# A two-layer encoder on one core: the second layer's plain x scaled at the layer's head, the decays loaded first, and the token sublayers in another order

## The chip, the cores and the metric

The kernel runs on one NeuronCore of a Trainium2 chip. The number of interest is the device time in microseconds (us) of one execution. The core has five engines that run side by side, each with its own instruction stream: TensorE (PE; its weight loads are listed as PEld), VectorE (DVE), ScalarE (ACT), GpSimd (POOL) and SyncE (SP). Data moves between the chip's memory (HBM) and the on-chip memory by DMA, issued here from the queues of SP and POOL. Matmul results land in eight PSUM banks.

## The reference

The trunk has two layers, on 512 tokens of width 1024. Each layer has a token sublayer and a channel sublayer, each followed by a residual addition with a factor alpha and a layer norm:

```python
for i in range(DEPTH):
    proj = x @ w_in[i]
    q_na, k_na, v_na, q_r, k_r, v_r, g_r, gate_a, gate_b = jnp.split(proj, IN_SPLITS, axis=-1)
    ya = neighbourhood_attention(...)          # 8 heads of 64, windows of 8 x 16
    yb = bidirectional_retention(...)          # 4 heads, group norm, times silu(g)
    merged = sigmoid(gate_a) * (ya @ w_branch_a[i]) + sigmoid(gate_b) * (yb @ w_branch_b[i])
    y = merged @ w_out[i]
    x = layer_norm(DEEPNORM_ALPHA * x + y, ln1_g[i], ln1_b[i])
    ffn = conv_glu_ffn(x, w_up[i], conv_w[i], conv_b[i], w_down[i])
    ple = jax.nn.sigmoid(x @ w_ple_gate[i]) * (p[i] @ w_ple_proj[i])
    x = layer_norm(DEEPNORM_ALPHA * x + ffn + ple, ln2_g[i], ln2_b[i])
```

The retention decays come from the inputs by a logarithm of a sigmoid, computed on the chip.

## The kernel before

**Arithmetic.** All operands are float32. Each is split into a high part `hi` (a cast, on ScalarE) and the rest `lo` (a subtraction, on VectorE), and each product is made of three matmuls: hi by hi, hi by lo, lo by hi (`mm3`, L434 to L436). A weight tile of 128 x 1024 is loaded from `wpack` into `raw`, split by `split` (L178, L179) and used by 12 or 24 matmuls. An item marked `sent` is split in another way (L392 to L394): ScalarE writes hi and minus hi, and a DMA issued by POOL adds the weight onto the latter, so VectorE does nothing for it.

**Blocks with sums.** Large products are done as blocks with seven products instead of eight, from sums of quarters of the operands (kinds a, c, t1, t2, d, t3, t4). For the weights, quarters are added by DMAs that accumulate in the tile (`rawa`, POOL's queue, L342). For the activations, `quad_sums` forms sums and splits them on VectorE and ScalarE.

**The stream of weights.** `Stream` lists all weight tiles in the order of use; `get` prepares a few tiles ahead of the one in use, and loads further ahead. A tile goes into a small pool of three, or, where a tuple such as `VG_HELD` or `BB_HELD` names it, into the unit pool (30 units of 128 x 1024), which lets it be prepared earlier.

**A token sublayer.** The head (`vg`) runs the keys of `VG[l]`: blocks 0 to 3 (values and gates, keys such as 3a, 2c) and plain products (nq, nk: queries and keys of the attention; q, k: of the retention, with rotary). Generators hang on the keys by `at_key`, and each call of one is a step: sums of x, the split of the second half of x, the decays, the tables of constants. In the head the engines run in the order in which the program is written (`_Ordered`, whose calls appear as L109). After it come the fillers in the order of `FILL[l]`, between which the steps of the attention heads (`NA_AT`) and of the retention heads (`RET_AT`) are placed by slot; here a scheduler orders each engine's instructions. The filler `ba` is the attention's branch product; after the fillers, `bb` is the retention's branch product in a block of seven, merged with the gates M (L1178, L1179), and turned by transpositions (`turn`, L1134). Then `proj_ln` makes the output projection with eight weight tiles, adds the residual `xn` and does LN1 (L506, L509).

**Plain x.** The residual needs x by rows. In layer 0 it is an input. In layer 1 it is LN2's output: at the end of layer 0, `norm` normalises R, four tiles of 128 x 1024, and each is stored without scale and shift into `x_scr`. In layer 1, in the middle of `bb` (step `XN_AT`), `plain_x` loads the constants and the four tiles and multiplies and adds on VectorE:

```python
                    nc.sync.dma_start(z, (scr if l else x_nat)[t * P:(t + 1) * P, :])
                    ...
                        nc.vector.tensor_mul(z, z, g)
                        nc.vector.tensor_add(z, z, b)
```

The transposed x of layer 1 is made from R apart from this (`out_pair`, with scale and shift on ScalarE), the first half at the end of layer 0, the second by `pending` at the head of layer 1.

**The start.** The first loads, in SP's queue, are p and its weights, x and the weights of block 3; the decays `dl` and `zd` are loaded by a step of `second_half`, and a later step computes their logarithms on VectorE with small instructions (`decay_logs`).

**The channel sublayer** (`pg`, up and down projections) is not touched.

Of the kernel before, what the change touches and what calls it, by code (L numbers as in the profile page):

```python
# [37 lines left out]
FILL = (('2c', '3t2', '3d', 'nk1', 'vn', '3t3', '3t4', '2t1', 'nk2', '2t2', '2d', '2t3', '0a', 'nq2', 'k2', '0t1', '2t4', '0t2', '0d', '0t3', '1a', 'q0',  # L38
# [9 lines left out]
OUT_PREP = ((0, 1, 1, 1), (0, 1, 1, 1))  # L48
# [32 lines left out]
VG_EARLY = 'd'  # L81
VG_HELD = (('0c', '0t2', '1a', '1c', '1t2', '1t4', '2a', '2t4', '3t1', '3t2'),
 ('0a', '0c', '0d', '0t3', '1c', '1t4', '2a', '2c', '2t1', '2t3', '3a', '3c', '3d', '3t1', '3t2', '3t3'))
# [42 lines left out]
def trunk(tc, wpack, x_nat, x_tr, head, p_tr, rpb, decay, ln_par, ln_col, conv, cos_t, sin_t, dist, xi_d, zd, ident_d, out):  # L126
# [4 lines left out]
    with ExitStack() as es:  # L131
# [103 lines left out]
        def vg_items(l):  # L235

            by = {}
            for b, c0 in enumerate((0, 12, 52, 36)):
                pos = {(q, j): (l, c0 + 2 * i + j, 0, 1024) for i, q in enumerate("acbd") for j in range(2)}
                for it in block_items(pos, {k[1:]: up for k in VG_HELD[l] if k[0] == str(b)}, VG_EARLY, ON_CHIP[l][b]):  # L240
                    it.block = b
                    by.setdefault(f"{b}{it.kind}", []).append(it)
            return [it for k in (*VG[l], *FILL[l]) for it in (by[k] if k in by else plain_items(l, k))]
# [19 lines left out]
        def bb_items(l):  # L263

            pos = {(q, j): (l, 44 + 2 * i + j, 0, 1024) for i, q in enumerate("acbd") for j in range(2)}
            by = {}
            for it in block_items(pos, {k: up for k in BB_HELD[l]}, BB_EARLY[l]):
                by.setdefault(it.kind, []).append(it)
            return [it for k in BB for it in by[k]]
# [34 lines left out]
        class Stream:  # L304


            def __init__(self):
                self.seq = []
                for l in range(DEPTH):
# [4 lines left out]
                    for c in range(64, 72):  # L314
                        plain(c)
                    self.seq += pg_items(l)
                    for s, n in enumerate(SEGS):
# [245 lines left out]
        for kp in range(2):  # L563
            x_load(0, kp)
            ws.load(3 + kp)
        ws.load(5)
        for kp in range(2):
            x_load(1, kp)
# [42 lines left out]

        NDL = DEPTH * 8
        lgs = cp.tile([P, NDL], F32, name="lgs")
        dl = cp.tile([P, NDL], F32, name="dl_0")
        nlg = cp.tile([P, NDL], F32, name="nlg")
# [69 lines left out]
        gscr = dp.tile([2, T, D], F32, name="g_scr")  # L685
        pending = None

        for l in range(DEPTH):
# [6 lines left out]
            def block(lh, emit):  # L695
# [61 lines left out]
                return step  # L757

            stores = []

# [160 lines left out]
            def ret_head(h):  # L921
# [39 lines left out]
                for tq in range(2):  # L961
# [17 lines left out]
                    for i in range(2):  # L979
                        y = yb[:, 2 * tq + i, :]  # L980
                        nc.vector.scalar_tensor_tensor(y, ps[:, i * 256:(i + 1) * 256], mv[:, i, 0:1], gg(2 * tq + i),
                                                       op0=ALU.subtract, op1=ALU.mult)
                        nc.vector.tensor_scalar_mul(y, y, r[:, i:i + 1])
                yield
# [132 lines left out]
            def plain_x():  # L1117

                if l:
                    g, b = ln_consts(l - 1, 1)  # L1120
                for t in range(4):
                    z = unit_f("xn")
                    nc.sync.dma_start(z, (scr if l else x_nat)[t * P:(t + 1) * P, :])
                    xn.append(z)
                    if l:
                        nc.vector.tensor_mul(z, z, g)
                        nc.vector.tensor_add(z, z, b)

# [87 lines left out]
            for i in range(n1 - 1, n1 + 3):  # L1216
                at_key(i, sums)
            if l == 0:
                rest, first = second_half(), first_half()
                at_key("p1", first)  # L1220
                at_key(0, first)
                at_key(2, ple_keep(l))
                tab = tables()
                for i in REST_AT:
                    at_key(i, rest)
                for i in TABLES_AT:
                    at_key(i, tab)
            else:
                rest = pending(2, xt, xf)
                at_key(1, ple_keep(l))  # L1230
                for i in PEND_AT:
# [19 lines left out]
            def fillers():  # L1251
                F = FILL[l]
                for i, f in enumerate(F):
                    if f == "vn":
                        yield from na_v()
                        continue
# [363 lines left out]
            for s, n in enumerate(SEGS):  # L1620
# [178 lines left out]
                for k in BOUND if not last else ("t4a", "t4b"):  # L1799
# [7 lines left out]
                    else:  # L1807
# [5 lines left out]
                        if not last:  # L1813
                            norm(i)
                            nc.sync.dma_start(scr[i * P:(i + 1) * P, :], R[i])
# [133 lines left out]
```

## Time and profile before

| | |
|---|---|
| time, median of 3 runs | 1685.13 us (1683.48 to 1687.44) |
| the profiled execution | 1689.1 us, with a span of 1687.3 us from the first to the last instruction |
| mean granted TensorE clock | 0.997 |
| busy: PE, DVE, ACT, POOL | 1656.4, 1314.1, 996.3, 232.2 us |
| moved by DMA | 324.13 MB, 192 GB/s |

The page gives the busy time of each engine and its costliest groups of instructions. A query by stretches gives the busy time in each, so that a full engine in one stage is seen where the average hides it. The list of waits says which engine waited for which, and the instructions in order of time show in brackets how long an engine had been idle and what ended that. A matmul's row lasts longer than the distance to the next one, since matmuls are pipelined.

### The profile page before, as it was taken

Reading aid. Unit: us, or ns where it says so; the run is one execution under the profiler, and the core shown is the slowest. Engines: PE = TensorE matmul, PEld = TensorE weight load, DVE = VectorE, ACT = ScalarE, POOL = GpSimd, SP = SyncE. Lnnn points to the kernel's source line nnn. Section 1 sums busy time; section 2 is a strip of 40 time slices with the busy share of each in tenths; the row PEclk is TensorE's granted clock in tenths of the full one; section 3 lists DMA queues with packets and bytes.
Section 4 is the critical chain, followed back from the end, with each engine's and each line's share of the span. In section 5 each row is a group of like instructions: output and inputs, shape, how many; then the busy total and the mean of one; then the engine's idle time right before and its main releaser. Section 6 shows DMA issues by size and latency. Waiting matters only on the chain.

```text
span 1687.3 us, 22720 instructions
## 1 busy us (share of the span) xinstructions
PE 1656.4 (98%) x8391; PEld 1399.0 (83%) x8391; DVE 1314.1 (78%) x2019; ACT 996.3 (59%) x1520; POOL 232.2 (14%) x277
## 2 busy tenths in 40 slices
PE   8999999999999999999999999999999999999997
PEld 6788888887888889789888888888877888898986
DVE  5847688979687867959976676788897887588598
ACT  5858876635266636546486888464533664474462
POOL 0102101110111111111111011010202111111112
PEclk9999999999999999999999999999999999999999
DMA  8857846556774788697686669544767767787874
GB/s 298 223 169 200 206 98 171 168 161 175 233 208 157 174 272 211 157 258 198 182 239 191 187 163 237 163 100 126 187 205 231 218 180 205 220 202 186 249 194 81
DMA packets 94719, 324.13 MB, mean 192 GB/s; under 512 B 10896, under 2 KB 11408, under 8 KB 94608
## 3 DMA queue, kind: packets, MB, share of 16 engines
q0 software_dynamic: 33840, 121.13, 36.7%
q1 hardware_dynamic: 60768, 201.55, 33.0%
q8 instruction: 66, 1.08, 0.2%
q14 instruction: 45, 0.37, 0.1%
HBM read 295.37 MB, written 26.21 MB: 191 GB/s over the span
## 4 chain that ended last, share of the span: by engine, by line
PE 59%; DVE 14%; issue 13%; DMA 8%; ACT 3%; POOL 1%; SPq 0%; DVEq 0%; POOLq 0%; ACTq 0%
PE u L435 4%; PE u L436 4%; PE u L434 4%; DMA rawa<-in_wpack 4%; PE gt L434 4%; PE gt L435 4%; PE gt L436 4%; PE gt L109 3%; DVE lo L179 3%; PE gn L436 3%; PE gn L434 3%; PE gn L435 3%; PE v L434 3%; PE v L436 3%; PE v L435 3%
## 5 line engine op out<-in xcount | busy, mean ns | idle before, releaser
L179 DVE TENSOR_TENSOR lo<-raw,hi 128x1024 fp32r<-128x1024 f32 (+1 forms) x156 | 188.9, 1217 | 97.6 <-ACT hi L178 97.0
L178 ACT CAST hi<-raw 128x1024 fp32r<-128x1024 f32 (+1 forms) x156 | 161.6, 1045 | 151.1 <-DMA raw<-in_wpack 57.7
L179 DVE TENSOR_TENSOR lo<-rawa,hi 128x1024 fp32r<-128x1024 f32 (+1 forms) x151 | 180.3, 1201 | 64.0 <-ACT hi L178 63.0
L178 ACT CAST hi<-rawa 128x1024 fp32r<-128x1024 f32 (+1 forms) x151 | 154.4, 1032 | 125.9 <-DMA rawa<-in_wpack 49.7
L342 POOL DMA_DIRECT2D rawa<-in_wpack x111 | 98.2, 885 | 624.9 <-DVE lo L179 481.7
L109 PE MATMUL gt<-x1t,hi 128*128 128x512 f32 x384 | 118.3, 389 | 0.0
L434 PE MATMUL gt<-x1t,hi 128*128 128x512 f32 x256 | 99.7, 390 | 0.0
L435 PE MATMUL gt<-x1t,hi 128*128 128x512 f32 x256 | 99.7, 390 | 0.0
L436 PE MATMUL gt<-x1t,lo 128*128 128x512 f32 x256 | 99.6, 389 | 0.0
L434 PE MATMUL gt<-xt,hi 128*128 128x512 f32 x216 | 84.7, 392 | 1.1 <-DVE t L886 0.7
L109 PEld LDWEIGHTS gt<-x1t,hi 128*128 128x128 f32 x384 | 72.1, 188 | 15.0
L435 PE MATMUL gt<-xt,hi 128*128 128x512 f32 x216 | 84.2, 390 | 0.0
L436 PE MATMUL gt<-xt,lo 128*128 128x512 f32 x216 | 84.2, 390 | 0.0
L342 POOL DMA_DIRECT2D rawt<-in_wpack x38 | 33.8, 890 | 309.7 <-DMA rawt<-in_wpack 116.2
L109 PE MATMUL gt<-x1t,lo 128*128 128x512 f32 x192 | 74.9, 390 | 0.1
L109 DVE TENSOR_TENSOR lo<-raw,hi 128x1024 fp32r<-128x1024 f32 (+1 forms) x46 | 54.5, 1197 | 5.2 <-ACT hi L109 4.9
L436 PEld LDWEIGHTS gt<-x1t,lo 128*128 128x128 f32 x256 | 48.1, 188 | 10.1
L434 PEld LDWEIGHTS gt<-x1t,hi 128*128 128x128 f32 x256 | 48.1, 188 | 9.6
L435 PEld LDWEIGHTS gt<-x1t,hi 128*128 128x128 f32 x256 | 48.1, 188 | 9.5
L179 DVE TENSOR_TENSOR lo<-rawt,hi 128x1024 fp32r<-128x1024 f32 (+1 forms) x36 | 42.8, 1193 | 14.8 <-ACT hi L178 14.6
L436 PE MATMUL gn<-hi,mt 128*128 128x512 f32 x128 | 49.3, 391 | 1.5 <-DVE mt L179 1.5
L435 PE MATMUL u<-lo,s 128*128 128x512 f32 x128 | 50.4, 394 | 0.0
(499 smaller groups left out, 5128.6 us busy)
## 6 DMA issues: line engine op xcount, KB each, us to landing
raw<-in_wpack SPq DMA_DIRECT2D x205, 512.0 KB, 4.8
rawa<-in_wpack POOLq DMA_DIRECT2D x124, 512.0 KB, 7.1
rawa<-in_wpack SPq DMA_DIRECT2D x42, 512.0 KB, 6.2
rawt<-in_wpack SPq DMA_DIRECT2D x42, 512.0 KB, 6.0
rawt<-in_wpack POOLq DMA_DIRECT2D x42, 512.0 KB, 7.6
s<-s_scr POOLq DMA_DIRECT2D x32, 512.0 KB, 11.7
s_scr<-s POOLq DMA_DIRECT2D x16, 512.0 KB, 5.1
r_scr<-pp SPq DMA_DIRECT2D x8, 512.0 KB, 10.6
```

The lines of the kernel that those rows point to most:

```text
L109: r = f(*a, **k)
L178: nc.scalar.copy(hi, src)
L179: nc.vector.tensor_sub(lo, src, _f(hi))
L342: nc.gpsimd.dma_start(it.raw[:, :w], wpack[l, c][:, o:o + w], accum_op=ALU.add)
L434: nc.tensor.matmul(ps, lh, rh, start=start, stop=False, skip_group_check=more)
L435: nc.tensor.matmul(ps, lh, rl, start=False, stop=False, skip_group_check=more)
L436: nc.tensor.matmul(ps, ll, rh, start=False, stop=stop, skip_group_check=more)
```

## The change

- `early_x`, at the head of layer 1, loads LN2's scale and shift, multiplies and adds in place on the tiles R that are still on the chip, and stores them to `x_scr`, step by step (`PX_AT`). The stores at the end of layer 0 go away, and `plain_x` in `bb` is left with four loads, in layer 1 at step 1 instead of 6, in layer 0 at 5 instead of 6.
- The decays and `zd` are loaded before the second half of x; their arithmetic and the splits of the second half follow in fewer steps (`REST_AT`). With `HOOK`, the first two of these steps run between the product of the first block's `a` and the copies of its result.
- `GN_ACT` names retention heads (three in layer 0, two in layer 1) whose group norm's last scaling goes from VectorE to ScalarE. `OUT_SENT` names output weights that are split with the help of a DMA (two a layer); `SENT` goes from two and five weights to four and four. `RC_ACT`, heads of the attention whose softmax is scaled on ScalarE, goes from six and three to three and five.
- `VG`, `FILL`, `RET_AT`, `NA_AT`, `VG_HELD`, `BB_HELD` and the places of the small steps have other values; steps can now lie among the fillers.

```diff
-SENT = (('k3', 'q2'), ('k2', 'k3', 'nk2', 'nq3', 'q1'))
+SENT = (('k0', 'nk0', 'q1', 'q3'), ('k2', 'nk3', 'nq2', 'q3'))
...
-RET_AT = ((33, 32, 38, 37), (31, 38, 36, 39))
-NA_AT = ((10, 13, 13, 16, 18, 19, 20, 23), (6, 9, 9, 10, 11, 11, 17, 20))
+RET_AT = ((28, 33, 38, 39), (35, 40, 38, 41))
+NA_AT = ((8, 10, 13, 16, 17, 18, 19, 21), (8, 11, 12, 12, 13, 14, 19, 22))
...
-VG = (('p0', 'p1', '3a', 'nq0', 'nk3', 'nq3', '3c', '3t1', 'nk0', '2a', 'nq1'), ('3a', '2a', '2c', '3c', '3t1', 'nq0', 'nk1', 'nk0', '3t2'))
-
-XN_AT = (6, 6)
-M_AT = (1, 5)
-TABLES_AT = (0, 6)
-REST_AT = (1, 1, 1, 1, 7, 8)
-PEND_AT = (1, 3)
+VG = (('p0', 'p1', '3a', 'nk3', 'nq0', '3c', 'nq3', '3t1', '2a', 'nk1', 'nq1'), ('3a', '2a', '2c', '3c', 'nq1', 'nk0', '3t1'))
+
+XN_AT = (5, 1)
+M_AT = (5, 5)
+TABLES_AT = (0, 12)
+REST_AT = (0, 0, 0, 1, 1, 6)
+SUM_AT = (-1, -3)
+PLE_AT = (0, 10)
+HOOK = (1, 1)
+PX_AT = (1, 3, 3, 3, 3, 6, 9, 9, 12)
+GN_ACT = ((1, 2, 3), (1, 3))
+BSENT = ((), ())
+OUT_SENT = ((5, 7), (4, 6))
+PEND_AT = (2, 3)
...
-BB_HELD = (('t2',), ('c', 'd', 't1', 't2', 't4'))
+BB_HELD = (('c', 'd'), ('c', 't2'))
...
-RC_ACT = ((0, 2, 3, 5, 6, 7), (3, 4, 6))
+RC_ACT = ((0, 1, 6), (0, 2, 3, 4, 6))
...
+        nc.sync.dma_start(dl, decay.to_broadcast([P, NDL]))
+        nc.sync.dma_start(zd_sb, zd)
         for kp in range(2):
             x_load(1, kp)
...
             ws.load(11)
-            nc.sync.dma_start(dl, decay.to_broadcast([P, NDL]))
-            nc.sync.dma_start(zd_sb, zd)
             yield
...
                         product(kind, st["u"], True)
+                        while hooks:
+                            next(hooks.pop(0))
                         st["p1"] = copies(st["u"], "p1")
...
-                        nc.vector.tensor_scalar_mul(y, y, r[:, i:i + 1])
+                        if h in GN_ACT[l]:
+                            nc.scalar.activation(y, y, AF.Copy, scale=r[:, i:i + 1])
+                        else:
+                            nc.vector.tensor_scalar_mul(y, y, r[:, i:i + 1])
...
             def plain_x():
 
-                if l:
-                    g, b = ln_consts(l - 1, 1)
                 for t in range(4):
                     z = unit_f("xn")
                     nc.sync.dma_start(z, (scr if l else x_nat)[t * P:(t + 1) * P, :])
                     xn.append(z)
-                    if l:
-                        nc.vector.tensor_mul(z, z, g)
-                        nc.vector.tensor_add(z, z, b)
+
+            def early_x():
+
+                g, b = ln_consts(l - 1, 1)
+                yield
+                for t in range(4):
+                    nc.vector.tensor_mul(RX[t], RX[t], g)
+                    yield
+                    nc.vector.tensor_add(RX[t], RX[t], b)
+                    nc.sync.dma_start(scr[t * P:(t + 1) * P, :], RX[t])
+                    yield
...
                         if not last:
                             norm(i)
-                            nc.sync.dma_start(scr[i * P:(i + 1) * P, :], R[i])
...
-            pending = out_pair
+            pending, RX = out_pair, R
```

More of the change, by code (lines that the diff above doesn't have):

```diff
@@ L36 @@
 DEEP = 5
-FILL = (('2c', '3t2', '3d', 'nk1', 'vn', '3t3', '3t4', '2t1', 'nk2', '2t2', '2d', '2t3', '0a', 'nq2', 'k2', '0t1', '2t4', '0t2', '0d', '0t3', '1a', 'q0',
[3 rows of a table removed]
+FILL = (('3d', '2c', '3t2', 'nk0', 'vn', '3t3', '2t1', 'nq2', '3t4', 'nk2', '2t2', '2d', '2t3', '0a', '2t4', '0t1', '0t2', 'k2', '0d', 'q0', '1a', '0t3',
[3 rows of a table added]
 BB = ("a", "c", "t1", "d", "t2", "t3", "t4")
-RET_AT = ((33, 32, 38, 37), (31, 38, 36, 39))
-NA_AT = ((10, 13, 13, 16, 18, 19, 20, 23), (6, 9, 9, 10, 11, 11, 17, 20))
+RET_AT = ((28, 33, 38, 39), (35, 40, 38, 41))
+NA_AT = ((8, 10, 13, 16, 17, 18, 19, 21), (8, 11, 12, 12, 13, 14, 19, 22))
 ORD = ('vector', 'scalar', 'tensor', 'gpsimd', 'sync')
@@ L81 @@
 VG_EARLY = 'd'
-VG_HELD = (('0c', '0t2', '1a', '1c', '1t2', '1t4', '2a', '2t4', '3t1', '3t2'),
- ('0a', '0c', '0d', '0t3', '1c', '1t4', '2a', '2c', '2t1', '2t3', '3a', '3c', '3d', '3t1', '3t2', '3t3'))
+VG_HELD = (('0t4', '1a', '1d', '2a', '2c', '3t2'), ('0t1', '0t3', '1t2', '1t4', '2a', '2c', '2t1', '2t3', '3a', '3c', '3d', '3t1', '3t3'))
 ON_CHIP = (('', '', 't2', ''), ('', '', '', ''))
-BB_HELD = (('t2',), ('c', 'd', 't1', 't2', 't4'))
+BB_HELD = (('c', 'd'), ('c', 't2'))
 BB_EARLY = ('a', 'a')
-RC_ACT = ((0, 2, 3, 5, 6, 7), (3, 4, 6))
+RC_ACT = ((0, 1, 6), (0, 2, 3, 4, 6))
 def _ap(t, off, dims):
@@ L241, in vg_items @@
                     it.block = b
+                    it.sent = f"{b}{it.kind}" in BSENT[l]
                     by.setdefault(f"{b}{it.kind}", []).append(it)
@@ L267, in bb_items @@
             for it in block_items(pos, {k: up for k in BB_HELD[l]}, BB_EARLY[l]):
+                it.sent = f"4{it.kind}" in BSENT[l]
                 by.setdefault(it.kind, []).append(it)
@@ L315, in __init__ @@
                         plain(c)
+                        self.seq[-1].sent = c - 64 in OUT_SENT[l]
                     self.seq += pg_items(l)
@@ L566, in trunk @@
         ws.load(5)
+        NDL = DEPTH * 8
+        lgs = cp.tile([P, NDL], F32, name="lgs")
+        dl = cp.tile([P, NDL], F32, name="dl_0")
+        nc.sync.dma_start(dl, decay.to_broadcast([P, NDL]))
+        nc.sync.dma_start(zd_sb, zd)
         for kp in range(2):
@@ L610, in tables @@
             yield
-        NDL = DEPTH * 8
-        lgs = cp.tile([P, NDL], F32, name="lgs")
-        dl = cp.tile([P, NDL], F32, name="dl_0")
         nlg = cp.tile([P, NDL], F32, name="nlg")
@@ L685, in trunk @@
         gscr = dp.tile([2, T, D], F32, name="g_scr")
-        pending = None
+        pending = RX = None
         for l in range(DEPTH):
@@ L757, in block @@
                 return step
+            hooks = []
             stores = []
@@ L1215, in trunk @@
             n1 = min(i for i, k in enumerate(keys) if k[1:] == "t1")
-            for i in range(n1 - 1, n1 + 3):
+            for i in range(n1 + SUM_AT[l], n1 + SUM_AT[l] + 4):
                 at_key(i, sums)
@@ L1221, in trunk @@
                 at_key(0, first)
-                at_key(2, ple_keep(l))
+                at_key(PLE_AT[0], ple_keep(l))
                 tab = tables()
-                for i in REST_AT:
+                for i in REST_AT[:2 if HOOK[0] else 0]:
+                    hooks.append(rest)
+                for i in REST_AT[2 if HOOK[0] else 0:]:
                     at_key(i, rest)
@@ L1229, in trunk @@
                 rest = pending(2, xt, xf)
-                at_key(1, ple_keep(l))
+                at_key(PLE_AT[1], ple_keep(l))
+                px = early_x()
+                for i in PX_AT:
+                    at_key(i, px)
                 for i in PEND_AT:
@@ L1253, in fillers @@
                 for i, f in enumerate(F):
+                    for g in steps.get(len(keys) + i, ()):
+                        next(g, None)
                     if f == "vn":
@@ L1814, in trunk @@
                             norm(i)
-                            nc.sync.dma_start(scr[i * P:(i + 1) * P, :], R[i])
                         elif i == 2:
```

2 lines of the change are left out of this document (1 added, 1 removed), and 6 rows, old and new, of the table FILL.

## The prediction

> **What bounds the kernel now.** I read the page's engine lines first, then the busy time by stage, then the list of who waited for whom on the TensorE, and last the instructions in order of time around the longest waits.
>
> ```profile
> span 1687.3 us, 22720 instructions
> ...
> PE 1656.4 (98%) x8391; PEld 1399.0 (83%) x8391; DVE 1314.1 (78%) x2019; ACT 996.3 (59%) x1520; POOL 232.2 (14%) x277
> ```
>
> TensorE is the bound: 98% busy, idle for 1687.3 - 1656.4 = 30.9 us. The change leaves its 8391 matmuls alone and only changes their order, so the gain can come out of these 30.9 us and out of matmuls at a reduced clock, and from nowhere else. Where the idle time lies, by stage (columns: stretch, length, busy PE, PEld, DVE, ACT, POOL with counts, clock, DMA share, GB/s):
>
> ```profile
> 0.00:75.00 75.00, 68.42 (x285) 52.80 (x286) 50.71 (x83) 47.66 (x73) 6.94 (x13) 1.00 0.84 258
> 100.00:250.00 150.00, 149.51 (x742) 125.03 (x741) 103.62 (x188) 115.89 (x218) 18.68 (x18) 1.00 0.59 149
> 375.00:425.00 50.00, 45.95 (x208) 37.03 (x207) 44.75 (x62) 26.77 (x38) 3.46 (x4) 0.97 0.63 182
> 850.00:925.00 75.00, 75.00 (x341) 62.36 (x340) 53.68 (x69) 54.98 (x85) 9.86 (x11) 1.00 0.85 234
> 1190.00:1290.00 100.00, 93.88 (x448) 76.49 (x447) 88.85 (x128) 41.10 (x58) 13.92 (x15) 1.00 0.72 206
> 1640.00:1688.00 48.00, 37.41 (x164) 30.32 (x162) 41.29 (x71) 14.23 (x17) 12.52 (x11) 0.93 0.45 94
> ```
>
> Three touched stages hold idle TensorE time: the start (6.6 us), layer 0's merge of the branches with the start of its output projection (375 to 425, 4.1 us), and the same in layer 1 (1190 to 1290, 6.1 us). In the two merges VectorE is the full engine: 44.75 of 50 and 88.85 of 100. At layer 1's head (850 to 925) it has 75 - 53.7 = 21.3 us free, and TensorE loses nothing there. The last stretch loses 10.6 us, and no edit reaches it. What TensorE waited for, start, first merge, second merge in turn:
>
> ```profile
> PE gt L109 <- DVE lo L109: 2.2, 1, 2.2
> PE gt L109 <- ACT xt L109: 1.2, 1, 1.2
> PE v L109 <- ACT s L109: 1.0, 1, 1.0
> PE w L435 <- DVE lo L109: 0.7, 1, 0.7
> ...
> PE u L435 <- DVE lo L179: 2.0, 1, 2.0
> PE tr L1134 <- DVE sa L1179: 1.6, 1, 1.6
> PE u L434 <- ACT u L710: 0.4, 1, 0.4
> ...
> PE tr L1298 <- DVE xn L509: 1.7, 1, 1.7
> PE gn L436 <- DVE mt L179: 1.5, 1, 1.5
> PE u L434 <- ACT mt L178: 1.2, 1, 1.2
> PE v L436 <- DVE yw L803: 0.7, 1, 0.7
> PE tr L1134 <- DVE sa L1179: 0.5, 1, 0.5
> PE u L436 <- DVE yw L803: 0.3, 1, 0.3
> ```
>
> They sum to 5.1, 4.0 and 5.9 us: nearly all the idle time, and nearly all of it is lateness of VectorE.
>
> **Part 1, the start: -4 us (bounds -5.1 and 0).** VectorE runs in program order here, so one late load holds all behind it (its instructions in order of time):
>
> ```profile
> 23.48 2.50 DVE L109 TENSOR_TENSOR xt<-xf,xt 128x512 fp32r<-128x512 f32 x4 [1.54 <-ACT xt L109]
> 32.99 0.18 DVE L109 TENSOR_SCALAR dl<-dl 128x16 f32<-128x16 f32 x1 [7.02 <-DMA dl<-in_decay]
> ...
> 36.56 1.22 DVE L109 TENSOR_TENSOR lo<-raw,hi 128x1024 fp32r<-128x1024 f32 x1
> ```
>
> VectorE stands idle 7.02 us for the decays, then runs sixteen small decay instructions, and only then the weight split `lo` (36.56) on which TensorE waits 2.2 us. In the changed program the decays and `zd` are the ninth and tenth loads of SP's queue, ahead of the last two loads of x, so the arithmetic starts as soon as x is split, and what stands behind it is a split due later. That wait goes. The 1.2 us wait is for the ScalarE casts of the second half of x, which stood behind the two copies of block 3a's product; the new hook runs them between the product and the copies, so it goes too, but for what TensorE catches up. The 1.0 us (sums of 3t1) gets the sublayer nq3 as cover, now placed ahead of it. 0.7 us (a `lo`) I leave out, since another `lo` may be late. 2.2 + 1.2 + 1.0 = 4.4; I take 4 for new small waits. What is late next: the decay arithmetic now runs in one piece, about 25 instructions or 5 us, and behind it stands the `lo` of 3c. The splits of x end at 26, so that `lo` ends near 32.2; TensorE has nk3 and nq0 to do first, 24 matmuls each, and without its wait starts them near 22.3 (rows of TensorE in order of time, and of the chain of waits for 48 such matmuls):
>
> ```profile
> 23.50 0.49 PE L109 MATMUL gt<-xt,hi 128*128 128x512 f32 x1 [1.19 <-ACT xt L109]
> ...
> 474.71 10.88 PE gt L109 x48
> ```
>
> It comes to 3c near 22.3 + 10.9 = 33.2. The cover is 1 us thick, and this is the part's risk. The two loads that went ahead cost SP two issues; the rotary tables move behind, and no rotary is due before the fillers.
>
> **Part 2, layer 0's merge: -3 us (bounds -5.6 and +2).** But for two splits of output weights at its end, nothing leaves VectorE here. The weights of `c` and `d` of the last branch projection are now held in the unit pool in place of those of `t2`, so their splits stand earlier, where VectorE idles (it is 89% busy over the merge, less before it), and the two `lo` of t2, which make the 2.0 us wait, stand less deep in the queue. The wait cost more than itself:
>
> ```profile
> 386.00:392.00 6.00, 4.19 (x11) 3.32 (x12) 6.00 (x9) 3.74 (x7) 1.73 (x2) 0.72 0.85 212
> 392.00:398.00 6.00, 6.00 (x28) 4.95 (x27) 3.85 (x5) 2.10 (x4) 0.00 (x0) 1.00 1.01 252
> ```
>
> Eleven matmuls where 28 fit: 11 x 6/28 = 2.4 us of work in 6 us, so 3.6 us lost, 2.0 by waiting and 1.6 because the granted clock was 0.72. If the wait goes, all 3.6 go. With the 0.4 and the 1.6 the stage has 5.6 us; the 1.6 (four multiplications and additions behind the last product, then a transposition) is a true chain and stays. I take -3, since the copies and constants around it are re-sorted as well. The lower bound for a loss, +2, is one more such wait. The Trainium skill's page "TensorE: Matmul & The Clock Gate", section "What's actually happening", says the clock halves after an idle window of about 3.4 us; here a wait of 2.0 us had that effect, and the trace decides. By the page alone the wait would be worth 2.0 us and not 3.6, and the sum -8.
>
> **Part 3, layer 1's merge: -4 us (bounds -5.9 and -1.5).**
>
> (First row from the chain of waits, then VectorE's instructions.)
>
> ```profile
> 1239.75 7.14 DMA xn<-x_scr
> ...
> 1246.98 1.23 DVE L1126 TENSOR_TENSOR xn<-xn,lng 128x1024 f32<-128x1024 f32 x1 [0.19 <-DMA xn<-x_scr]
> ...
> 1255.06 0.68 DVE L179 TENSOR_TENSOR mt<-tr,mt 128x512 fp32r<-128x512 f32 x1
> 1255.66 1.22 DVE L1127 TENSOR_TENSOR xn<-xn,lnb 128x1024 f32<-128x1024 f32 x1
> 1256.79 1.88 DVE L179 TENSOR_TENSOR mt<-tr,mt 128x512 fp32r<-128x512 f32 x3
> ```
>
> Eight multiplications and additions by LN2's scale and shift, 9.9 us from 1246.98 to 1256.88, stand in a row on the full engine, and the splits `mt` that the output projection needs wait behind them: the 1.5 us wait is theirs whole. All eight leave; `plain_x` becomes four loads, issued at the merge's second step instead of its seventh. Five heads' scaling in the group norm also goes to ScalarE (two of them here), and two output weights are split with the help of a DMA. So VectorE's 88.85 us fall by some 12. The waits for `yw` (0.7, 0.3), `mt` (1.2) and `sa` (0.5) are of the same lateness; I count 1.5 + 1.2 + 0.7 + 0.3 + 0.5 = 4.2, rounded to 4. The 1.7 us wait for the layer norm of the last row tile is a chain and stays. At worst only the 1.5 goes.
>
> **Part 4, layer 1's head: +1 us (bounds 0 and +4).** The eight instructions, two loads of constants and four stores arrive here. VectorE has room, and a hole at the very place:
>
> ```profile
> 866.24 1.23 DVE L179 TENSOR_TENSOR lo<-raw,hi 128x1024 fp32r<-128x1024 f32 x1 [7.72 <-ACT hi L178]
> ...
> lng<-in_ln_par SPq DMA_DIRECT2D x4, 512.0 KB, 6.5
> lnb<-in_ln_par SPq DMA_DIRECT2D x4, 512.0 KB, 7.6
> ```
>
> The first multiplication stands in program order ahead of the `lo` at 866.24. The constants are issued just before the hole of 7.72 us opens and land 6.5 and 7.6 us later, so they about fit into it. Then five of the eight, 6 us, stand ahead of the second `lo` of 3c; by my count it comes within half a microsecond of its matmul. If the constants need 12 us instead (DMA share is 0.85 here), 4 us are lost. The four stores leave the end of layer 0 and come here, and the four of the embedding's product keep their place, so bytes in flight at the head do not grow much. SP's weight loads stand behind the stores, which wait for VectorE; a late addition would delay them, and the hole in VectorE is what covers that.
>
> **Part 5, the re-sorted middle of both sublayers: +1 us (bounds -2 and +10).**
>
> ```profile
> L983 DVE TENSOR_SCALAR yb<-yb,rstd x32: 342/350/362, 307.2 to 1198.4; 128x256 f32<-128x256 f32 x32
> ...
> L393 ACT ACTIVATE lo<-hi x7: 1042/1062/1067, 268.3 to 1120.6; 128x1024 fp32r<-128x1024 f32 x7
> ...
> 189.07 1.28 ACT L770 ACT_TABLE_LOAD   x1
> 190.37 0.60 ACT L770 ACTIVATE sg<-u 128x512 f32<-128x512 f32 x1
> ```
>
> VectorE gives 20 group-norm scalings (0.35 us each, 7 us) and takes four of the softmax back; five more weight tiles are split by ScalarE and an accumulating load instead of VectorE, 5 x 1.06 us onto ScalarE and five more DMAs on POOL, whose queue also carries the `rstd` powers. Counting the changed program's order, sigmoid, silu and exp alternate more often: 49 table loads instead of 41, 8 x 1.28 = 10.2 us more on ScalarE, six of them in layer 0, five of these between 100 and 250. There ScalarE is busy 115.89 of 150 us, so there is cover; gone, it would cost up to those 10.2. On the good side stand at most the 2 us of waits outside the three stages. I take +1. The Trainium skill's page "ScalarE: Activation LUTs", section "What ACT_TABLE_LOAD costs", gives 2.66 us for each switch with its drain; in this trace the next activation starts 0.02 us after the 1.28 us load. By the page the eight would be 21.3 us, more than the stage's slack shares out easily.
>
> **Sum.** -4 -3 -4 +1 +1 = -9 us. The profiled execution took 1689.1 us with a span of 1687.3; it becomes 1680. It lies 4 us above the median of the runs, 1685.1, so the median becomes 1676.
>
> **Rivals.**
> - *The scaling is late at layer 1's head.* Constants land after the hole, VectorE starts the layer 4 us behind: part 4 at its bound and a wait or two carried on, -9 + 4 = -5, 1680. For it: DMA share 0.85, program order. Against: 21.3 us of free VectorE.
> - *The full engine stays full.* In layer 0's merge nothing is removed, so the wait comes back at another product; part 2 gives 0, the start gives half, part 3 its -1.5, part 4 and 5 their +1: -2 - 1.5 + 2 = -1.5, about 1684. For it: 44.75 of 50 on VectorE. Against: the free VectorE time before the merge.
> - *ScalarE becomes the bound in layer 0's middle*, the case on the other side. Between the branches' sigmoids and the softmax each of the added table loads stands in front of an activation for which TensorE waits. It decides where 10 us of new waiting, half-rate stretches included, fall on TensorE; with all of the 10.2 us and a stretch of 1.6 us after two or three of them it is -10 + 10.2 + 4 = +4, 1689. For it: 115.89 of 150 busy before the loads. Against: TensorE now idles 0.5 us there with seven such loads.
>
> **How the numbers follow.** The forecast has 0.58, the late scaling 0.16, the full engine 0.10, ScalarE 0.13, and 0.03 for a larger gain than my sum. The runs of the kernel before lie within 4 us, so 0.2% (3.4 us) is about what can be told from no change. Faster: 0.58 + 0.16 + 0.03 = 0.77; same 0.10; slower 0.13. The forecast's own range is 1670 to 1681; 1668 to 1687 takes in the next two and leaves out the ScalarE case and the largest gains.
>
> **What the profile of the changed kernel would show.** Start: no idle of VectorE for `dl`, less than 3 us of TensorE idle beyond the first gap. Layer 0's merge: clock 1.00 throughout. Layer 1's merge: no `xn` by `lng` on VectorE, its busy time under 80 of 100, TensorE idle about 2 us. Head of layer 1: the first `R` by `lng` ends before 867 less the gain so far; a TensorE wait for `lo` of 3c would be the late scaling. Between 100 and 250: TensorE idle over 3 us with ScalarE as releaser would be the third rival. The prediction is wrong if waits of 2 us or more appear at new places, each with its half-rate stretch.

## The result, and the profile after

The changed kernel takes 1693.95 us (median of 16 runs, 1687.71 to 1696.74) against 1686.05 us of the kernel before, measured beside it: the ratio is 1.0042 with a 95% interval of 1.0031 to 1.0053. It is slower; the forecast was 1676.

The profiled execution of it took 1687.7 us and is the quickest of its 16 runs, so the places of the loss are seen in it but not their whole size. Its page, engine lines:

```profile
span 1685.9 us, 22741 instructions
...
PE 1655.3 (98%) x8391; PEld 1400.0 (83%) x8391; DVE 1303.9 (77%) x1998; ACT 1018.0 (60%) x1549; POOL 235.0 (14%) x282
```

VectorE lost 10 us of work and ScalarE gained 22; the prediction counted items of both and gave no total for the execution. Busy time by stretch of the changed kernel (columns as in the prediction), and then one stretch of the kernel before that the prediction did not show:

```profile
0.00:75.00 75.00, 73.75 (x315) 58.71 (x316) 56.63 (x89) 55.04 (x83) 8.51 (x15) 1.00 0.95 302
100.00:250.00 150.00, 148.79 (x752) 125.52 (x751) 109.86 (x208) 119.04 (x214) 19.64 (x19) 1.00 0.62 160
350.00:375.00 25.00, 22.97 (x127) 19.58 (x125) 16.94 (x32) 14.18 (x23) 5.63 (x7) 1.00 0.76 188
375.00:425.00 50.00, 47.72 (x222) 38.98 (x223) 45.52 (x64) 28.27 (x39) 2.81 (x4) 1.00 0.71 206
850.00:925.00 75.00, 70.79 (x312) 57.84 (x310) 56.40 (x66) 48.24 (x73) 7.34 (x9) 0.98 0.81 239
1190.00:1290.00 100.00, 95.63 (x463) 78.56 (x462) 76.39 (x113) 46.05 (x69) 15.59 (x17) 1.00 0.78 224
```

```profile
350.00:375.00 25.00, 25.00 (x137) 21.59 (x136) 17.61 (x35) 10.33 (x14) 3.47 (x5) 1.00 0.63 170
```

The start is 5.3 us better (68.42 to 73.75 of 75), the merge of layer 0 has its clock back (0.97 to 1.00), and the merge of layer 1 is 1.75 us better with VectorE at 76 instead of 89. Against that stand 2.0 us of idle TensorE just ahead of layer 0's merge, and 4.2 us at layer 1's head, both places where it lost nothing before, and a wait of 2.4 us at 85 us, between the stretches shown. From 100 to 250 us, where the prediction looked for its ScalarE rival, TensorE idles 1.2 us instead of 0.5, and the longest wait there (1.0 us, for `ya`) is for VectorE. The list of waits of the changed kernel names who was late:

```profile
PE u L444 <- DVE lo L185: 3.8, 2, 3.1
PE w L443 <- ACT yw L184: 3.4, 2, 2.4
PE tr L1155 <- DVE sa L1200: 2.8, 2, 1.7
PE gt L445 <- DMA lo<-in_wpack: 2.4, 1, 2.4
...
PE gt L444 <- DVE xt L185: 1.1, 1, 1.1
PE ns L1079 <- DVE ya L1121: 1.0, 1, 1.0
```

Three waits of 2.4 to 3.1 us are new. In order of time, TensorE's instruction behind each:

```profile
85.45 0.50 PE L445 MATMUL gt<-xt,lo 128*128 128x512 f32 x1 [2.42 <-DMA lo<-in_wpack]
...
375.37 0.50 PE L443 MATMUL w<-hi,yw 128*128 128x512 f32 x1 [2.40 <-ACT yw L184]
...
899.71 0.50 PE L444 MATMUL u<-lo,s 128*128 128x512 f32 x1 [3.10 <-DVE lo L185]
```

**At 85 us: nk0.** This weight is now split with the help of a DMA. The DMA is issued at 75.25 (POOL's row), and the summary of DMA issues between 70 and 90 us gives 10.2 us to its landing, with the DMA engines full (a busy share of 1.03 from 75 to 85 us):

```profile
75.25 0.86 POOL L403 DMA_DIRECT2D lo<-in_wpack  x1 [0.58 <-ACT lo L402]
...
lo<-in_wpack POOLq DMA_DIRECT2D x1, 512.0 KB, 10.2
```

75.25 + 10.2 = 85.45: the matmul starts in the moment in which the weight lands.

**At 375 us: head 3 of the retention.** It now starts two slots later, at 39. Its result Y is copied and cast by ScalarE, which by then has the weights of the merge in hand. The last transposition that makes Y ends at 370.3; ScalarE, which has just stood idle for 2.23 us until a sum of weights landed, casts weights and copies a product first (ScalarE's instructions):

```profile
369.92 1.05 ACT L184 CAST hi<-rawa 128x1024 fp32r<-128x1024 f32 x1 [2.23 <-DMA rawa<-in_wpack]
370.87 1.05 ACT L184 CAST hi<-raw 128x1024 fp32r<-128x1024 f32 x1
371.82 1.07 ACT L719 COPY p<-u 128x512 f32<-128x512 f32 x2
372.77 1.08 ACT L1006 COPY Y<-ybt 128x512 f32<-128x512 f32 x2
373.73 1.08 ACT L184 CAST hi<-raw 128x1024 fp32r<-128x1024 f32 x1
374.67 0.65 ACT L184 CAST yw<-Y 128x512 fp32r<-128x512 f32 x1
```

**At 900 us: 3t2 of layer 1.** Before, three products (nq0, nk1, nk0) lay between 3t1 and 3t2; now one does, nk1. A weight of 3t2 is a sum that an accumulating DMA makes, and that DMA is issued only when VectorE has split the weight before it. The chain, in rows of VectorE, POOL and ScalarE, in order of time:

```profile
883.23 1.22 DVE L185 TENSOR_TENSOR lo<-rawa,hi 128x1024 fp32r<-128x1024 f32 x1
...
884.74 0.86 POOL L351 DMA_DIRECT2D rawa<-in_wpack  x1 [5.00 <-DVE lo L185]
...
893.59 1.05 ACT L184 CAST hi<-rawa 128x1024 fp32r<-128x1024 f32 x1 [2.41 <-DMA rawa<-in_wpack]
...
898.44 2.35 DVE L185 TENSOR_TENSOR lo<-rawa,hi 128x1024 fp32r<-128x1024 f32 x2
```

Split, issue, 8.9 us to the cast of what landed, and 3.8 us more until VectorE has the sums of the activations behind it. The theory for the experiments was therefore: the re-sorted orders, and for nk0 the split with the help of a DMA, took the cover (the TensorE work that hides a preparation) from three operands; each costs its wait and sometimes a stretch at half clock. The rival was that ScalarE's added work (prediction's last rival) delays the middle in many small places.

### The profile page after: what moved, and what is told of

Its sections match the earlier page's. It is cut to its first block, busy times and chain, and to the rows that moved or that the text cites. A ratio compares the mean times of both kernels' runs of the same rounds, so it can differ in the third digit from the quotient of the medians.

```text
span 1685.9 us, 22741 instructions
## 1 busy us (share of the span) xinstructions
PE 1655.3 (98%) x8391; PEld 1400.0 (83%) x8391; DVE 1303.9 (77%) x1998; ACT 1018.0 (60%) x1549; POOL 235.0 (14%) x282
## 4 chain that ended last, share of the span: by engine, by line
PE 63%; DVE 14%; DMA 11%; issue 6%; ACT 5%; POOL 1%; SPq 0%; DVEq 0%; POOLq 0%; ACTq 0%
PE gt L115 8%; DMA rawa<-in_wpack 6%; PE u L444 5%; PE u L445 4%; PE gt L445 4%; PE gt L443 4%; PE gt L444 4%; PE u L443 4%; DVE lo L185 4%; PE u L115 3%; PE v L443 3%; PE v L445 3%; PE v L444 3%; PE gn L445 2%; PE gn L443 2%
## 5 line engine op out<-in xcount | busy, mean ns | idle before, releaser
L185 DVE TENSOR_TENSOR lo<-raw,hi 128x1024 fp32r<-128x1024 f32 x149 | 179.8, 1215 | 101.0 <-ACT hi L184 100.1
L184 ACT CAST hi<-raw 128x1024 fp32r<-128x1024 f32 x149 | 154.5, 1045 | 156.1 <-PE gt L444 60.9
L115 DVE TENSOR_TENSOR lo<-raw,hi 128x1024 fp32r<-128x1024 f32 (+1 forms) x48 | 56.9, 1199 | 7.3 <-ACT hi L115 7.2
L115 ACT CAST hi<-raw 128x1024 fp32r<-128x1024 f32 (+1 forms) x48 | 48.9, 1031 | 5.7 <-PE u L115 3.0
```

The costliest lines, as they stand in the source:

```text
L115: r = f(*a, **k)
L184: nc.scalar.copy(hi, src)
L185: nc.vector.tensor_sub(lo, src, _f(hi))
```

## The experiments

All ratios are to the kernel before, measured beside each group of runs; they compare means, while the times given are medians. Layer by layer first.

**The changed kernel once more.** No edit.

> The changed kernel once more, for a second profile: its profiled execution was the quickest of sixteen, 6 us under their median. Theory A (the scaling at layer 1's head comes late): the slower executions lose more in the head of layer 1, 850 to 925, TensorE idle there 6 us or more instead of 4.2. Theory B (the new order leaves too little time for loads that add onto a tile, some 9 us each): the slower executions wait for such loads at several places, in both layers. Theory C (table loads on ScalarE): waits with ScalarE as releaser between 100 and 250. Ratio to the kernel before 1.004 in all three.

Measured: 1692.36 us, 1.0043 (1.0028 to 1.0058). The loss repeats. In this profile too TensorE waits for the same three operands, at 85, 379 and 904 us (2.0, 2.0 and 3.0 us), each time with a stretch at half clock behind it, and a fourth wait of 2.3 us stands at 210 us, for `ya`. The head of layer 1 idles 4.0 us, no more than in the first profile, which speaks against theory A, though this profile too (1689.7 us) is the quickest of its runs.

**Layer 0 sorted as before.** Only the early load of the decays stays; layer 1 as changed.

```diff
-RET_AT = ((28, 33, 38, 39), (35, 40, 38, 41))
-NA_AT = ((8, 10, 13, 16, 17, 18, 19, 21), (8, 11, 12, 12, 13, 14, 19, 22))
+RET_AT = ((33, 32, 38, 37), (35, 40, 38, 41))
+NA_AT = ((10, 13, 13, 16, 18, 19, 20, 23), (8, 11, 12, 12, 13, 14, 19, 22))
...
```

(and in the same way the first entry of each of the other tuples)

> Layer 0 has all settings of the kernel before (order, held tiles, heads on ScalarE, steps), but for the early load of the decays; layer 1 stays as changed. If the loss lies in layer 1 (theory A, or theory B in layer 1), the ratio is 1.006 or more, since the gain of 5 us at the start is undone. If it lies in layer 0 (theory C, or B in layer 0), the ratio is 1.000 or less.

Measured: 1686.88 us, 1.0012 (1.0003 to 1.0021). So layer 0's changes bring about 5 us of the loss, although part of the gain of the start is theirs; the 2 us that stay go with layer 1, where the wait for 3t2's `lo` is still there (2.9 us).

**Layer 1 sorted as before**, with the scaling in the merge; layer 0 as changed.

```diff
-RET_AT = ((28, 33, 38, 39), (35, 40, 38, 41))
+RET_AT = ((28, 33, 38, 39), (31, 38, 36, 39))
...
-                px = early_x()
-                for i in PX_AT:
-                    at_key(i, px)
```

> Layer 1 has all settings of the kernel before, and its plain x is scaled in the merge again; layer 0 stays as changed. Theory A and B in layer 1: faster than the kernel before by 3 to 5 us, ratio 0.997 to 0.998, from the start. Theory C or B in layer 0: 1.003 or more.

Measured: 1690.65 us, 1.0032 (1.0019 to 1.0045). That is some 2 us less than `again`, but the intervals overlap, so layer 1's part, the scaling included, isn't shown to be a loss by this run: its gains in the merge went away together with its late operand.

**The scaling alone.** The kernel before with `early_x` and nothing else of the change.

```diff
+                px = early_x()
+                for i in PX_AT:
+                    at_key(i, px)
...
-                    if l:
-                        nc.vector.tensor_mul(z, z, g)
-                        nc.vector.tensor_add(z, z, b)
```

> The kernel before with one part of the change: plain x scaled at layer 1's head from the tiles on chip, at the same step numbers. Theory A: slower, 3 to 6 us (1.002 to 1.004), with VectorE idle for the constants and TensorE waiting for a weight split between 860 and 900. Theory B: about 2 to 4 us faster (0.998), since the merge of layer 1 loses its wait of 1.5 us and more and the order of the products is that of before.

Measured: 1685.36 us, 1.0001 (0.9991 to 1.0011): nothing, which neither theory expected. The merge's waits for VectorE's `mt` (1.5 us) and for the last row's `xn` (1.7 us) are gone from its list, and the merge idles 2.5 us instead of 6.1; two others stand at layer 1's head, which idles 3.7 us instead of none:

```profile
PE w L441 <- DVE lo L182: 1.8, 1, 1.8
PE gt L442 <- DMA lo<-in_wpack: 1.7, 1, 1.7
```

```profile
850.00:925.00 75.00, 71.26 (x320) 58.26 (x319) 59.00 (x71) 50.94 (x78) 8.44 (x9) 1.00 0.86 249
1190.00:1290.00 100.00, 97.50 (x472) 80.56 (x471) 83.75 (x126) 44.24 (x66) 14.79 (x15) 1.00 0.76 225
```

The first has its cause in VectorE's rows: the constants land late, VectorE stands idle for them for 9.8 us, and the split that TensorE needs comes behind three scaling instructions. For the second, late loads behind the stores of x are the likely cause, which was not tried apart:

```profile
863.74 2.36 DVE L1141 TENSOR_TENSOR R<-R,lng 128x1024 f32<-128x1024 f32 x2 [9.80 <-DMA lng<-in_ln_par]
866.02 1.22 DVE L1143 TENSOR_TENSOR R<-R,lnb 128x1024 f32<-128x1024 f32 x1
867.15 1.22 DVE L182 TENSOR_TENSOR lo<-raw,hi 128x1024 fp32r<-128x1024 f32 x1
```

**The late operands, one by one, out of the changed kernel.** First nk0 split on VectorE again.

```diff
-SENT = (('k0', 'nk0', 'q1', 'q3'), ('k2', 'nk3', 'nq2', 'q3'))
+SENT = (('k0', 'q1', 'q3'), ('k2', 'nk3', 'nq2', 'q3'))
```

> The changed kernel with one weight of layer 0, nk0, split by VectorE again instead of with the help of a DMA; all else as changed. Theory A (covers lost: the loss is a few places where one operand now comes 2 to 3 us late, each with a possible half-rate stretch behind it): the wait of 2.1 to 3.0 us for that weight at 82 us goes, and in most executions 1.7 us of half-rate TensorE with it; -2 to -4 us against the changed kernel, ratio to the kernel before 1.002 to 1.003. Theory B (ScalarE's added table loads and scalings spread small delays over layer 0's middle): no place matters by itself, the ratio stays at 1.004.

Measured: 1687.85 us, 1.0005 (0.9993 to 1.0016). The wait is gone, and the gain, some 6 us by the ratios, is more than the 2 to 4 expected. Next, 3t2 of layer 1 behind nq0:

```diff
- ('nk1', '3t2', 'nq0', 'nk2', '3d', '3t3', ...
+ ('nk1', 'nq0', '3t2', 'nk2', '3d', '3t3', ...
```

> The changed kernel with the block product 3t2 of layer 1 behind nk1 and nq0 instead of behind nk1 alone; all else as changed. Theory A: the wait of 3.1 us at 897 us goes, since the weight sums that DMAs add up have 5.4 us more, and the half-rate stretch behind it too; -3 to -4.7 us against the changed kernel, ratio 1.0015 to 1.0025. If instead the late scaling on VectorE is what holds the head of layer 1, not the place of 3t2, the wait turns up at another operand, and the ratio stays at 1.004.

Measured: 1687.63 us, 1.0001 (0.9990 to 1.0012). The wait is gone and no other took its place; the gain, some 7 us by the ratios, is again more than expected (3 to 4.7). Then layer 0's last head at its slot of before:

```diff
-RET_AT = ((28, 33, 38, 39), (35, 40, 38, 41))
+RET_AT = ((28, 33, 38, 37), (35, 40, 38, 41))
```

> The changed kernel with the start of layer 0's last retention head at slot 37 instead of 39, as in the kernel before; all else as changed. Theory A: the wait of 2.1 to 2.6 us for yw in layer 0's merge (373 us) goes; -2 to -4 us against the changed kernel, ratio 1.002 to 1.003. Theory B: ScalarE is full and the head only moves its work, no change, 1.004.

Measured: 1692.55 us, 1.0034 (1.0022 to 1.0045). Not told from no change by this run: the wait of 2.4 us is gone, but four of 0.3 to 0.5 us stand in its place (the same four of fixed_again are shown below). And all three edits together:

> The three edits together. Theory A: the places are apart in time, so the gains add up: -7 to -12 us against the changed kernel, ratio 0.997 to 1.000. Theory B: no better than 1.003.

Measured: 1682.25 us, 0.9969 (0.9958 to 0.9981). This beats both kernels, with ScalarE's work of the changed kernel unaltered: its busy time is 1017.3 us against 1018.0, and with the same 49 table loads. One of their groups, with the same line in the changed kernel and in three_fixes:

```profile
L912 ACT ACT_TABLE_LOAD x6 | 7.7, 1283 | 0.1
```

So the rival, ScalarE's added loads, falls as the cause of the loss. That they cost nothing at all isn't shown: no run takes them out alone.

**Around the repaired program.** Four more questions. First the kernel before with the scaling alone, one key later:

```diff
-PX_AT = (1, 3, 3, 3, 3, 6, 9, 9, 12)
+PX_AT = (1, 4, 4, 4, 5, 6, 8, 9, 10)
```

> The kernel before with the scaling of x moved to layer 1's head, as in early_x_alone, but its multiplications and additions placed one key later and closer together, behind the splits for 3c. If the waits of 1.9 us at 866 us (lo behind the scaling) and at 921 us (a sent weight, whose loads stand in SP's queue behind the late stores of x) are what takes back the gain of the merge, they go, and the time falls by 3 to 4 us below early_x_alone: ratio 0.998. If the head is simply too full for the eight instructions, other waits come in their place, ratio 1.000.

Measured: 1686.68 us, 1.0001 (0.9988 to 1.0013). A miss: in the trace the same two multiplications and an addition still stand ahead of the late split, and TensorE waits 2.1 us for it; the wait for the sent weight fell from 1.7 to 0.7 us. In the trace the edit moved only later instructions, so it does not say whether the head is too full. Second, the scaling back in the merge of three_fixes:

```diff
-XN_AT = (5, 1)
+XN_AT = (5, 6)
...
-                px = early_x()
...
+                        nc.vector.tensor_mul(z, z, g)
+                        nc.vector.tensor_add(z, z, b)
```

> The kernel three_fixes with the scaling of x back in layer 1's merge (plain_x at step 6, stores at the end of layer 0). What moving the scaling is worth in this program: by the prediction's parts 3 and 4, and by the three waits of VectorE in the merge that came back in layer1_old (2.6 and 1.9 us and 1.3 us), 3 to 5 us slower than three_fixes, ratio 0.999 to 1.000. If the scaling is neutral here as it was alone, 0.997.

Measured: 1689.63 us, 1.0016 (1.0004 to 1.0028), some 8 us more than three_fixes, twice what was expected. Its list has the wait for `mt` that the prediction put down to the scaling, and a second one at the head, where ScalarE stands idle for 6.8 us until a weight lands. That the stores of x, which lie ahead of that weight's load in SP's queue there, delay it is argued from their order and was not tried apart:

```profile
PE w L443 <- ACT xf L1773: 3.3, 1, 3.3
...
PE gn L445 <- DVE mt L185: 2.3, 1, 2.3
```

Third, layer 0 sorted as before, layer 1 as changed with 3t2 later (the edits of layer0_old and t2_later together):

> Layer 0 sorted as before (with the decays loaded early), layer 1 as changed but with 3t2 behind nq0: the better half of each. layer0_old gave 1.0012 with a wait of 3.1 us for lo at 898 us; that wait and its half-rate stretches of 3.4 us go: ratio 0.996 to 0.998. If layer 0's changed sort has a gain of its own beside its waits, this stays above three_fixes (0.9969).

Measured: 1683.87 us, 0.9980 (0.9970 to 0.9990). As good as three_fixes within the intervals, so layer 0's new order has no clear gain of its own once its late operands are mended. Last, three_fixes with two smaller waits attacked as well:

```diff
-NA_AT = ((8, 10, ...
+NA_AT = ((9, 10, ...
-PX_AT = (1, 3, 3, 3, 3, 6, 9, 9, 12)
+PX_AT = (1, 4, 4, 5, 5, 6, 9, 9, 12)
```

> three_fixes and two more: the first attention head of layer 0 one slot later (its wait of 1.2 to 1.6 us for ya at 205 us), and the scaling's steps one key later (the wait of 1.1 us for xt at 875 us). Both waits are under 2 us, behind which no run showed a half-rate stretch, so only they themselves are to be had: -1 to -2.5 us against three_fixes, ratio 0.9955 to 0.9965. If waits only move on, 0.997.

Measured: 1684.79 us, 0.9986 (0.9977 to 0.9996). A miss: both waits (1.6 us for `ya`, 1.1 us for `xt`) stand in its trace as before, and nothing is gained.

**Each late operand put back into the repaired program**, measured side by side, so that their prices can be compared. The yardstick, three_fixes again:

> The program three_fixes once more, as the yardstick of this call. If late operands are the cause: ratio 0.996 to 0.998, as the first time. If the first time was luck of its chip: above 0.999.

Measured: 1682.02 us, 0.9969 (0.9958 to 0.9981). Its two longest waits, and its stretches:

```profile
PE tr L1155 <- DVE sa L1200: 2.8, 2, 1.7
PE tr L1326 <- DVE xn L518: 1.2, 1, 1.2
```

```profile
350.00:375.00 25.00, 24.23 (x114) 19.64 (x113) 16.53 (x25) 15.04 (x22) 5.04 (x6) 1.00 0.88 224
375.00:425.00 50.00, 47.16 (x218) 37.93 (x218) 42.58 (x60) 25.94 (x35) 2.59 (x3) 1.00 0.70 216
850.00:925.00 75.00, 73.89 (x334) 60.87 (x333) 60.70 (x72) 51.36 (x78) 7.12 (x9) 1.00 0.82 248
1190.00:1290.00 100.00, 96.25 (x453) 78.42 (x453) 77.82 (x108) 47.25 (x73) 14.88 (x15) 1.00 0.76 220
```

No single wait reaches 2 us. With nk0 split by the DMA again:

```diff
-SENT = (('k0', 'q1', 'q3'), ...
+SENT = (('k0', 'nk0', 'q1', 'q3'), ...
```

> three_fixes, with the weight nk0 split with the help of a DMA again. A wait of 2 to 4 us for it at 83 us, with a half-rate stretch (1.7 us lost) in most executions: +3.5 to +5.5 us above fixed_again. By the first comparison (wait taken away from the changed kernel) +6.

Measured: 1686.39 us, 1.0000 (0.9991 to 1.0010): +4.4 us by the medians. With 3t2 right behind nk1:

```diff
- ('nk1', 'nq0', '3t2', 'nk2', ...
+ ('nk1', '3t2', 'nq0', 'nk2', ...
```

> three_fixes, with 3t2 right behind nk1 again. A wait of 3 us for lo at 896 us, with one or two half-rate stretches: +4 to +6 us above fixed_again. By the first comparison +7.

Measured: 1685.93 us, 0.9995 (0.9985 to 1.0005): +3.9 us. With head 3 late:

```diff
-RET_AT = ((28, 33, 38, 37), ...
+RET_AT = ((28, 33, 38, 39), ...
```

> three_fixes, with layer 0's last retention head at slot 39 again. The profile of head3_earlier had four waits of 0.4 to 0.7 us where the changed kernel has one of 2.2 to 2.6, so the lateness only splits up and what goes is the half-rate stretch: 0 to +2 us above fixed_again.

Measured: 1685.06 us, 0.9992 (0.9982 to 1.0002): +3.0 us, more than was expected. The intervals of nk0_back and t2_back lie clear of that of fixed_again, the one of head3_back only just; by these intervals each price is uncertain by 2 to 3 us. The three waits, as TensorE's instruction behind each shows them (one row for each kernel):

```profile
85.87 0.50 PE L445 MATMUL gt<-xt,lo 128*128 128x512 f32 x1 [2.75 <-DMA lo<-in_wpack]
```

```profile
899.63 0.50 PE L444 MATMUL u<-lo,s 128*128 128x512 f32 x1 [3.25 <-DVE lo L185]
```

```profile
373.76 0.50 PE L443 MATMUL w<-hi,yw 128*128 128x512 f32 x1 [2.29 <-ACT yw L184]
```

In fixed_again the last one is split up, because ScalarE's casts and VectorE's subtractions of the merge are still behind, one operand after the other:

```profile
373.04 0.50 PE L443 MATMUL v<-hi,yw 128*128 128x512 f32 x1 [0.51 <-ACT yw L812]
374.04 0.50 PE L445 MATMUL v<-hi,yw 128*128 128x512 f32 x1 [0.26 <-DVE yw L815]
380.63 0.50 PE L443 MATMUL u<-hi,yw 128*128 128x512 f32 x1 [0.43 <-ACT yw L812]
382.32 0.50 PE L445 MATMUL u<-hi,yw 128*128 128x512 f32 x1 [0.50 <-DVE yw L815]
```

4.4 + 3.9 + 3.0 = 11.3 us; with the 5.0 us by which fixed_again lies below the kernel before, the changed kernel should lie 6.3 us above it. It lies 7.9 and 7.7 us above in its two comparisons. By means instead of medians the three cost 14.2 us and fixed_again lies 5.5 below, so it should lie 8.7 us above; measured are 7.1 and 7.2. Within this noise the three operands account for the loss.

## Why the prediction was wrong

**Part 1, the start (-4): right.** The idle time of TensorE in the first 75 us fell by 5.3 us, there is no wait for the decays, and the thin cover of 3c held. The size is that of one execution, though: with the old start TensorE idles 6.6, 3.3 and 6.2 us in the three profiles that have it (before, early_x_alone, early_x_later), since the decays come 7.0, 2.1 and 6.7 us late; with the new one it idles 1.3 to 2.6 us in thirteen profiles.

**Part 2, layer 0's merge (-3): right in its stage in one profile, taken back just ahead of it.** From 375 to 425 the idle time fell from 4.05 to 2.28 us and the half-rate stretch (1.6 us) went, 3.4 us together. But the 2.0 us that 350 to 375 lost belong to the same merge: its first products wait for head 3. In the second profile (again) head 3's wait falls inside the stage, which idles 3.9 us, with a half-rate stretch behind that wait; in fixed_again 350 to 425 still idles 3.6 us, without one. The part looked at VectorE, and the late engine was ScalarE. The prediction's reading that nearly all the idle time is lateness of VectorE was too strong: of the 15.0 us in its three lists, ScalarE is named for 3.8.

**Part 3, layer 1's merge (-4): the mechanism right, the size only in the order of before.** merge_x shows the wait for `mt` behind the scaling, and in early_x_alone the stage idles 3.6 us less. With layer 1 re-sorted the stage won 1.75 us (changed kernel) and 2.4 (fixed_again), not 4: the wait for `sa` became longer (1.7 us instead of 0.5), although VectorE has 24 us free there. It is 0.5 us in early_x_alone and 1.7 in old0_t2_later, so it came with layer 1's new order.

**Part 4, layer 1's head (+1, bounds 0 and +4): right only in the changed program's company.** The scaling costs at most 1.1 us there (the new wait for `xt`). Alone, in the order of before, it took back the whole gain of the merge (3.7 us lost, 3.6 won), half of it by the mechanism of the rival "the scaling is late" (1.8 us), the rest by the wait for a sent weight (1.7 us). That the worth of the scaling depends on the order around it, nothing alone and 8 us in three_fixes, was not in the prediction at all.

**Part 5, the re-sorted middle (+1, bounds -2 and +10): the step that failed.** It priced what the re-sort adds on ScalarE, table loads above all, and let the lost covers cost nothing. They cost 11.3 us: nk0, whose split now waits for a DMA that takes 10.2 us there (+4.4), 3t2 with one product ahead of it instead of three (+3.9), head 3 two slots later (+3.0). Where cover was lost stands in the tuples of the diff. How much was needed could be had only roughly from the trace of before, where a weight that an accumulating DMA splits lands in 7.5 us by the median.

From -9 to the measured +7.9 us are 16.9 us. This part's term accounts for 10.3 of them (11.3 instead of 1). Another 5.0 are the other four parts': they were forecast at -10 together, and the program that has them without the three late operands, but with the rest of the re-sort, gained 5.0 (fixed_again). The profile of before from which the sum starts lies 4 us above its median, part 1 was sized by a late load that is not as late in every run, and the new order of layer 1 took back some of part 3; how these share the 5.0 stays open. The 1.6 us that are left lie within the noise.

The sentence that the prediction would be wrong "if waits of 2 us or more appear at new places, each with its half-rate stretch" is what happened, but for the "each": one of the three waits in the first profile had a stretch behind it, all three in the second.

## What to carry to other kernels

When an order is re-sorted, don't price the moved instructions alone: for each operand that is prepared by a DMA or by a chain of engines, count how many products now lie between the moment its preparation may start and its use, before and after. On an engine that is 98% busy, three operands that lost their cover ate more than twice what the rest of the change gained (11.3 against 5.0 us). Here a wait shortened below 2 us was worth more than its length, since no half-rate stretch came behind the shorter ones. That a long wait split into short ones is already a gain rests on head3_back alone (+3.0 us); out of the changed kernel the same edit gave no clear gain.

## What the runs showed of the clock

A wait of TensorE may or may not be followed by a stretch at half clock, and the same kernel shows both. Three waits of the changed kernel's profile, 5 us behind each; then nk0_back behind its wait:

```profile
85.40:90.40 5.00, 4.95 (x22) 4.07 (x23) 0.00 (x0) 0.00 (x0) 0.00 (x0) 1.00 1.01 340
375.40:380.40 5.00, 5.00 (x22) 4.13 (x23) 5.00 (x8) 2.42 (x4) 0.85 (x1) 1.00 1.00 315
899.70:904.70 5.00, 4.99 (x15) 3.98 (x16) 4.93 (x5) 1.87 (x3) 2.62 (x3) 0.66 0.61 97
```

```profile
86.70:90.10 3.40, 3.40 (x10) 2.67 (x9) 0.00 (x0) 0.00 (x0) 0.00 (x0) 0.51 1.02 369
90.10:93.50 3.40, 3.40 (x17) 2.80 (x16) 0.00 (x0) 0.90 (x1) 0.00 (x0) 1.00 0.25 96
```

A stretch is 3.4 us long at 0.5, which costs 1.7 us. Over the 18 profiled executions of this study there are 110 waits of TensorE of 0.8 to 1.9 us between the start and the last stage, none with such a stretch behind it, and 30 of 1.96 to 3.7 us, 18 with one. One of these stretches, in layer0_old, begins 2.1 us into a wait of 2.9 us and lasts 6.8 us. The stretches are one reason why the changed kernel's runs lie apart: its profile with one took 1687.7 us, its second profile (again) with three took 1689.7. The whole 9 us between its quickest and its slowest run are not explained by that; no slow one of them was profiled. The Trainium skill's page "TensorE: Matmul & The Clock Gate", section "What's actually happening", has the gate watch windows of about 3.4 us that run freely, whatever the kernel does. The length of the stretch agrees (3.4 us), and that the same wait is punished in one execution and not in the next fits windows that don't follow the kernel; but waits of 2.0 us were enough here, so the idle time need not fill a window.
